# One decoder block on one core: the three late token operands of the up projection start at byte 160 of a 256-byte line, as the other four do

## The chip, the core and the metric

The kernel runs on one core of one Trainium2 chip. The metric is the device time of one execution in microseconds; the time before is the median of three runs. TensorE (PE) multiplies, and loads the stationary operand of each product with a separate weight load (PEld). VectorE (DVE), ScalarE (ACT) and GpSimd (POOL) prepare operands and take results away, and SyncE (SP) and POOL start the transfers.

## The reference, cut to what matters

One decoder block over 512 tokens of width 2048: an input projection, four heads of gated linear attention, four heads of differential attention, an output projection, and a gated MLP of width 5632 with a causal convolution of three taps.

```python
h = rmsnorm(x, attn_pre_norm);  m = token_mixer(h, w_in, ..., w_o)
x = x + rmsnorm(m, attn_post_norm)
h = rmsnorm(x, ffn_pre_norm)
up = h @ w_ffn_in                        # 2048 -> 2 * 5632
a, b = up[..., :5632], up[..., 5632:]
f = (gelu(conv3(a)) * b) @ w_ffn_out     # 5632 -> 2048
x = x + rmsnorm(f, ffn_post_norm)
```

## The kernel before, in words

Every large product is made of three: an fp32 operand is split into a rounded part (hi, written by ACT) and a rest (lo, by DVE), and hi·hi, hi·lo and lo·hi are summed in PSUM. The tokens stand as `ah` and `al` (L70, L71), 128 x (4 token tiles, 16 k tiles, 128), 32 KB in a partition each. Weights come in granules of 512 KB (`load` L96, `load_t` L817) into four buffers `raw` or four `rt`, and `granule` (L101) splits each into `whi` and `wlo` of 1024 columns, of which there are three each; in places every fourth granule goes to a spare pair, `xhi` and `xlo`. The order of the instructions on each engine is fixed when the program is built.

Which operand moves through the array and which stands in it differs by stage. In the profile's names, `bank<-A,B` has the moving operand first.

- `mm_n` (L160 to L166) in `proj_n`: the weights move, 512 columns in one piece; a slice of `ah` or `al` of 128 columns stands. It makes the value and gate parts of the input projection and the whole output projection. A granule is 24 matmuls, of which six belong to each token tile. `to_ffn` (L616) calls it in an order of its own, six matmuls for a granule and token tile.
- `mm_t` (L138 to L148) in `proj_t`: the tokens move, four blocks of 128 columns (one of each token tile, 8192 bytes apart); the weights stand. It makes queries and keys and the first of the up projection. A granule is 24 matmuls. In `to_ffn` the same function runs with two token tiles, so two blocks and 256 columns.
- `forget_gate` (L346) multiplies the moving `ah` and `al`, again four blocks, into 16 slices of `gas`, 80 columns wide and 320 bytes apart (L360, L361).
- `up_prods` (L885 to L895): the up projection, as products of 2 x 2 blocks with seven instead of eight block products (Strassen's scheme in Winograd's form). The tokens move, two blocks of 128 columns; the weights stand. Four of the seven token operands are quarters of `ah` and `al` (`a11`, `a12`, `s7`, `a22`: two blocks 8192 bytes apart). The three others, `s5`, `s2` and `s3`, are tiles of their own (L776), hi and lo each 8 KB, with the two blocks 4096 bytes apart; `up_sums` (L780) writes them. A unit (L826) has seven segments of two granules, one for each token operand, in the order y0 (`s2`), z1 (`s3`), x1 (`a12`), y1 (`s7`), the next unit's x0 (`a11`), y2 (`a22`), and the next unit's z0 (`s5`). A segment is 2 granules x 2 columns halves x 4 k tiles x 3 = 48 matmuls, and there are 20 units.
- `down_prods` (L984 to L992): the down projection, by the same scheme. The weights move, 512 columns in one piece; slices of `ah` and `al` stand. A granule is 12 matmuls; every fourth granule is `xhi`, `xlo`. `ffn_out_part` (L1091 to L1099) does the same for the last group.

All tiles are laid out by pools, one behind the other in a partition. The pool `small` (L59) stands behind `ah` and `al` and ahead of `w` (L63: `raw`, `whi`, `wlo`), `rp` (`rt`), `fa` (L727: `s5`, `s2`, `s3`, the unit's result tiles) and, in its place later, `ff`. So a byte more or less in `small` moves all that follows.

```python
ss = small.tile([P, 2], F32, name="ss2", tag="ss2")           # L216, eight buffers of 32 bytes
rp = ctx.enter_context(tc.tile_pool(name="rp", bufs=4))       # L725
fp = fa.enter_context(tc.tile_pool(name="fa", bufs=2))        # L727
for n in ("s5", "s2", "s3"):                                  # L776
    up[n] = tuple(fp.tile([P, 2, HK, P], F32R, name=f"{n}{v}", bufs=1) for v in "hl")
```

Of the kernel before, what the change touches and what calls it, by code (L numbers as in the profile page):

```python
# [9 lines left out]
F32 = mybir.dt.float32  # L10
# [7 lines left out]
P = 128  # L18
# [17 lines left out]
def hybrid_layer(ctx: ExitStack, tc: tile.TileContext, x, attn_pre_norm, w_in, w_alpha_up, b_alpha,  # L36
# [3 lines left out]
    nc = tc.nc  # L40
# [6 lines left out]
    def dma(o, i):  # L47
        return nc.sync.dma_start(out=o, in_=i)
# [10 lines left out]
    small = ctx.enter_context(tc.tile_pool(name="small", bufs=8))  # L59
# [13 lines left out]
    def bank(pool=None):  # L73
        return (pool or psa).tile([P, 512], F32, name="bank", tag="bank")
# [21 lines left out]
    def load(src, a):  # L96
        raw = wpool.tile([P, GR], F32, name="raw", tag="raw", bufs=4)
        dma(raw.rearrange("p (a b) -> p a b", a=a), src)
        return raw

    def granule(src, a, raw=None, spare=None, bufs=4):  # L101
        if raw is None:
            raw = load(src, a)
        if spare:
            hi = spare.tile([P, GR], F32R, name="xhi", tag="xhi", bufs=bufs)
            lo = spare.tile([P, GR], F32R, name="xlo", tag="xlo", bufs=bufs)
        else:
            hi = wpool.tile([P, GR], F32R, name="whi", tag="whi")
            lo = wpool.tile([P, GR], F32R, name="wlo", tag="wlo")
        act(hi, raw, AF.Copy)  # L110
        tt(lo, raw, hi.bitcast(F32), ALU.subtract)  # L111
        r = "p (a b) -> p a b"
        return hi.rearrange(r, a=a), lo.rearrange(r, a=a)

    def rsqrt_mean(ss, n, width=1):
        t = small.tile([P, width], F32, name="ms", tag="ms")
        nc.gpsimd.tensor_scalar(t, ss, 1.0 / n, EPS, ALU.mult, ALU.add)
        r = small.tile([P, width], F32, name="rs", tag="rs")
        nc.gpsimd.tensor_tensor(r, t, nhalf[:, :width], ALU.pow)
        return r  # L120
# [5 lines left out]
    def transpose_into_act(src, t, slot0, n):  # L126
        for g in range(0, n, 4):
            m = min(4, n - g)
            b = bank()
            for j in range(m):  # L130
                nc.tensor.transpose(b[:, j * P:(j + 1) * P], src[:, (g + j) * P:(g + j + 1) * P], ident)  # L131
            bv = b[:, :m * P].rearrange("p (k c) -> p k c", k=m)
            split(ah[:, t, slot0 + g:slot0 + g + m, :], al[:, t, slot0 + g:slot0 + g + m, :], bv)

    def bcast_row(tile_ap, row):
        dma(tile_ap, row.partition_broadcast(P))
# [23 lines left out]
    def mm_n(banks, t, g, w):  # L160
        for k in range(2):
            s = 2 * g + k
            st, sp = s == 0, s == KT - 1
            mm(banks[t], ah[:, t, s, :], w[0][:, k, :], start=st, stop=False)  # L164
            mm(banks[t], ah[:, t, s, :], w[1][:, k, :], start=False, stop=False)  # L165
            mm(banks[t], al[:, t, s, :], w[0][:, k, :], start=False, stop=sp)  # L166
# [17 lines left out]
    def big8(name):  # L184
        return mx.tile([P, 2048], F32, name=name, tag="big8", bufs=6)
# [8 lines left out]
    def first_half(c):  # L194
        gb = big8("gb")
        jb = mx.tile([P, 1024], F32, name="jb", tag="jb", bufs=1)
        xts = [big8("xt") for _ in range(NT)]
        H2 = [slice(1024 * i, 1024 * (i + 1)) for i in range(2)]
        H4 = [slice(512 * i, 512 * (i + 1)) for i in range(4)]
        rs, raws, w = {}, {}, {}  # L200
        banks = [bank(psm) for _ in range(NT)]
        col = C_GV + 512 * c

        def load_x(t):
            for i in range(2):
                dma(xts[t][:, H2[i]], x2[t * P:(t + 1) * P, H2[i]])

        def load_w(*gs):
            for g in gs:
                raws[g] = load(w_in3[:, 2 * g:2 * g + 2, col:col + 512], 2)  # L210

        def weights(g):
            w[g] = granule(None, 2, raws[g], spare=mx if g == 3 else None, bufs=1)

        def square(t):
            ss = small.tile([P, 2], F32, name="ss2", tag="ss2")  # L216
            for i in range(2):
                act(jb, xts[t][:, H2[i]], AF.Square, accum_out=ss[:, i:i + 1])
            sm = small.tile([P, 1], F32, name="ss", tag="ss")
            nc.gpsimd.tensor_tensor(sm, ss[:, 0:1], ss[:, 1:2], ALU.add)  # L220
            rs[t] = rsqrt_mean(sm, D)

        def scale(t, *ps):
            for i in ps:
                stt(xts[t][:, H4[i]], xts[t][:, H4[i]], rs[t], gb[:, H4[i]], ALU.mult, ALU.mult)

        def turn(t, *ps):
            for i in ps:
                transpose_into_act(xts[t][:, H4[i]], t, 4 * i, 4)

        def prods(t, *gs):
            for g in gs:
                mm_n(banks, t, g, w[g])

        load_x(0)
        bcast_row(gb[:, H2[0]], attn_pre_norm[0, H2[0]])
        load_w(0, 1, 2)
        load_x(1)
        load_w(3)
        load_x(2)  # L240
        load_x(3)
        bcast_row(gb[:, H2[1]], attn_pre_norm[0, H2[1]])
        square(0)
        scale(0, 0, 1)
        weights(0)
        turn(0, 0, 1)
        weights(1)
        weights(2)
        square(1)
        prods(0, 0, 1)  # L250
        scale(1, 0, 1)
        prods(0, 2)
        weights(3)
        turn(1, 0, 1)
        square(2)
        prods(0, 3)
        square(3)
        scale(2, 0, 1)
        prods(1, 0, 1, 2)
        turn(2, 0, 1)  # L260
        prods(1, 3)
        scale(3, 0, 1)
        prods(2, 0, 1)
        turn(3, 0, 1)
        scale(0, 2, 3)
        prods(2, 2)
        turn(0, 2, 3)
        scale(1, 2, 3)
        prods(2, 3)
        turn(1, 2, 3)  # L270
        scale(2, 2, 3)
        prods(3, 0, 1)
        turn(2, 2, 3)
        scale(3, 2, 3)
        prods(3, 2)
        turn(3, 2, 3)
        prods(3, 3)
        return banks
# [446 lines left out]
    rp = ctx.enter_context(tc.tile_pool(name="rp", bufs=4))  # L725
    fa = ExitStack()
    fp = fa.enter_context(tc.tile_pool(name="fa", bufs=2))  # L727
    ud0 = dram.tile([P, 4, S], F32, name="ud0")
    SN = ("a11", "a12", "a22", "s5", "s2", "s7", "s3")
    sd = [{n: dram.tile([P, 2, S], F32, name=f"sd{c}{n}") for n in SN} for c in range(NG // 2)]  # L730
# [460 lines left out]
```

## Time and profile before

| | us |
|---|---|
| median of 3 runs (lowest to highest) | 2177.14 (2175.53 to 2177.21) |
| the profiled execution's own time | 2177.07 |
| its span, first to last instruction | 2175.4 |
| PE busy in the span | 2140.5 (98%) |
| DVE busy | 1418.5 (65%) |
| ACT busy | 901.4 (41%) |
| POOL busy | 204.8 (9%) |

The granted clock of TensorE is 0.996 over the span. In time the stages are: the first projection up to 126 us, the mixer's projections with the attention work in their gaps up to 625, the output projection up to 845, the passage to the MLP and the first up products up to 937, the up units from 937 to 1725, the down units to 2113, and the last group to the end.

How to read it: a matmul's record in the profile is longer than the time that it keeps the array, since matmuls follow each other in a pipeline; what counts is the distance from one start to the next. In a timeline, the first column is the start in us from the span's beginning, and the second the record's length. A row of the grouped view has the line, engine, operation, tiles, shapes and count, then busy us and the mean ns of one record, then the idle time before.

### The profile page before, as it was taken

To read this page: it belongs to the slowest core of one execution; us is meant where nothing else is said; L and a number is where in the kernel's file an instruction comes from. 1 tells how busy PE (TensorE), PEld (TensorE's weight loads), DVE (VectorE), ACT (ScalarE), POOL (GpSimd) and SP (SyncE) were. 2 spreads that over 40 slices of the span, in tenths; PEclk is the share of its full clock that TensorE was granted. 3 is DMA by queue.
4 is the path that set the end of the run, shared out by engine and by line. 5 is a ranking of instruction groups with operands and counts; after the bars stand their busy time and mean duration, and the time that the engine had idled before them with its cause. 6 is when DMAs were issued, how large, how long until landed. Compare 5 with 4: busy or idle time off the path is not lost.

```text
span 2175.4 us, 31878 instructions
## 1 busy us (share of the span) xinstructions
PE 2140.5 (98%) x13009; PEld 1893.4 (87%) x13009; DVE 1418.5 (65%) x1721; ACT 901.4 (41%) x1162; POOL 204.8 (9%) x245
## 2 busy tenths in 40 slices
PE   7999999999999999999999999999999899999997
PEld 6778888787888888899999999999999788788886
DVE  5345554443444237688777786777777777888987
ACT  4233332333343224344444544444444464444433
POOL 1000000000000001011111111111011011111101
PEclk9999999999999999999999999999999999999999
DMA  6322222223224335365776757667577677576653
GB/s 212 101 71 78 78 69 78 78 78 84 77 83 167 95 126 184 126 133 129 162 169 152 163 142 181 155 144 183 140 168 181 180 212 211 167 194 174 172 157 136
DMA packets 218472, 303.83 MB, mean 140 GB/s; under 512 B 11777, under 2 KB 155573, under 8 KB 216405
## 3 DMA queue, kind: packets, MB, share of 16 engines
q1 hardware_dynamic: 165204, 238.87, 33.6%
q0 software_dynamic: 53120, 62.92, 18.6%
q8 instruction: 102, 1.67, 0.3%
q14 instruction: 46, 0.37, 0.0%
HBM read 273.97 MB, written 27.79 MB: 139 GB/s over the span
## 4 chain that ended last, share of the span: by engine, by line
PE 50%; issue 43%; POOL 3%; DVE 2%; DMA 1%; ACT 1%; POOLq 0%; SPq 0%; DVEq 0%; ACTq 0%
PE bank L164 7%; PE bank L166 7%; PE bank L165 6%; PE bank L148 5%; PE bank L146 5%; PE bank L147 5%; PE bank L991 3%; PE bank L992 3%; PE bank L990 3%; POOL rt L842 2%; POOL raw L842 2%; PE bank L413 1%; PE bank L481 1%; PE bank L512 1%; PE bank L131 1%
## 5 line engine op out<-in xcount | busy, mean ns | idle before, releaser
L111 DVE TENSOR_TENSOR wlo<-raw,whi 128x1024 fp32r<-128x1024 f32 x307 | 374.4, 1222 | 363.1 <-ACT whi L110 353.0
L110 ACT ACTIVATE whi<-raw 128x1024 fp32r<-128x1024 f32 x307 | 324.8, 1059 | 604.2 <-PE bank L166 160.3
L895 PE MATMUL bank<-ah,wlo 128*128 128x256 f32 x1280 | 353.7, 276 | 0.4 <-DVE wlo L111 0.4
L893 PE MATMUL bank<-ah,whi 128*128 128x256 f32 x1280 | 353.6, 276 | 0.0
L894 PE MATMUL bank<-al,whi 128*128 128x256 f32 x1280 | 353.4, 276 | 0.0
L111 DVE TENSOR_TENSOR wlo<-rt,whi 128x1024 fp32r<-128x1024 f32 x220 | 267.9, 1221 | 94.9 <-ACT whi L110 94.8
L110 ACT ACTIVATE whi<-rt 128x1024 fp32r<-128x1024 f32 x220 | 232.3, 1059 | 229.8 <-PE bank L894 171.5
L895 PEld LDWEIGHTS bank<-ah,wlo 128*128 128x128 f32 x1280 | 240.2, 188 | 0.8 <-DVE wlo L111 0.8
L893 PEld LDWEIGHTS bank<-ah,whi 128*128 128x128 f32 x1280 | 240.4, 188 | 0.1
L894 PEld LDWEIGHTS bank<-al,whi 128*128 128x128 f32 x1280 | 240.3, 188 | 0.1
L164 PE MATMUL bank<-whi,ah 128*128 128x512 f32 x600 | 238.4, 400 | 0.6 <-ACT ah L123 0.6
L165 PE MATMUL bank<-wlo,ah 128*128 128x512 f32 x600 | 236.5, 395 | 0.0
L166 PE MATMUL bank<-whi,al 128*128 128x512 f32 x600 | 236.3, 396 | 0.0
L146 PE MATMUL bank<-ah,whi 128*128 128x512 f32 (+1 forms) x512 | 198.0, 387 | 0.0
L147 PE MATMUL bank<-al,whi 128*128 128x512 f32 (+1 forms) x512 | 196.6, 384 | 0.0
L148 PE MATMUL bank<-ah,wlo 128*128 128x512 f32 (+1 forms) x512 | 196.6, 384 | 0.0
L991 PE MATMUL bank<-wlo,ah 128*128 128x512 f32 x420 | 164.8, 393 | 1.5 <-DVE wlo L111 1.5
L992 PE MATMUL bank<-whi,al 128*128 128x512 f32 x420 | 164.7, 393 | 0.0
L990 PE MATMUL bank<-whi,ah 128*128 128x512 f32 x420 | 156.1, 390 | 0.3 <-DVE acc L998 0.3
L166 PEld LDWEIGHTS bank<-whi,al 128*128 128x128 f32 x600 | 113.1, 189 | 25.6 <-DVE al L124 0.3
L165 PEld LDWEIGHTS bank<-wlo,ah 128*128 128x128 f32 x600 | 113.2, 189 | 24.9 <-DVE wlo L111 0.5
L164 PEld LDWEIGHTS bank<-whi,ah 128*128 128x128 f32 x600 | 113.1, 189 | 24.4 <-ACT ah L123 1.0
(250 smaller groups left out, 4103.9 us busy)
## 6 DMA issues: line engine op xcount, KB each, us to landing
raw<-in_w_in_dram SPq DMA_DIRECT2D x96, 512.0 KB, 3.8
raw<-in_w_ffn_in_dram SPq DMA_DIRECT2D x96, 512.0 KB, 4.7
raw<-in_w_ffn_out_dram SPq DMA_DIRECT2D x48, 512.0 KB, 5.8
rt<-in_w_ffn_in_dram SPq DMA_DIRECT2D x40, 512.0 KB, 6.3
rt<-in_w_ffn_in_dram POOLq DMA_DIRECT2D x40, 512.0 KB, 6.1
raw<-in_w_ffn_in_dram POOLq DMA_DIRECT2D x40, 512.0 KB, 7.0
raw<-in_w_o_dram SPq DMA_DIRECT2D x32, 512.0 KB, 3.8
rt<-in_w_ffn_out_dram SPq DMA_DIRECT2D x20, 512.0 KB, 7.2
```

Source lines behind the costliest of these rows:

```text
L110: act(hi, raw, AF.Copy)
L111: tt(lo, raw, hi.bitcast(F32), ALU.subtract)
L146: mm(o, wh, ah[:, t0:t1, kk, :], start=st, stop=False)
L147: mm(o, wh, al[:, t0:t1, kk, :], start=False, stop=False)
L148: mm(o, wl, ah[:, t0:t1, kk, :], start=False, stop=sp)
L164: mm(banks[t], ah[:, t, s, :], w[0][:, k, :], start=st, stop=False)
L165: mm(banks[t], ah[:, t, s, :], w[1][:, k, :], start=False, stop=False)
L166: mm(banks[t], al[:, t, s, :], w[0][:, k, :], start=False, stop=sp)
L893: mm(o, wh, sh[:, :, kk, :], start=start and kk == 0 and n == 0, stop=False, **NOW)
L894: mm(o, wh, sl[:, :, kk, :], start=False, stop=False, **NOW)
L895: mm(o, wl, sh[:, :, kk, :], start=False, stop=kk == HK - 1, **NOW)
L991: mm(b[j], sh[:, o:o + P], w[1][:, q, :], start=False, stop=False, **NOW)
```

## The change

`ss2` has four buffers instead of eight, which takes 4 x 32 = 128 bytes out of `small`; a tile `pad` of 80 floats, 320 bytes, which nothing reads, stands ahead of everything else in `fa` and is set to zero once by DVE. No other instruction is added, removed or moved on any engine.

```diff
@@ first_half, square
-            ss = small.tile([P, 2], F32, name="ss2", tag="ss2")
+            ss = small.tile([P, 2], F32, name="ss2", tag="ss2", bufs=4)
@@ hybrid_layer
     rp = ctx.enter_context(tc.tile_pool(name="rp", bufs=4))
     fa = ExitStack()
     fp = fa.enter_context(tc.tile_pool(name="fa", bufs=2))
+
+    pad = fp.tile([P, 80], F32, name="pad", bufs=1)
+    nc.vector.memset(pad, 0.0)
     ud0 = dram.tile([P, 4, S], F32, name="ud0")
```

On DVE, where `up_sums` begins (L791), the rows of before are these; the names in brackets are the semaphores waited for.

```order
578 L111 TENSOR_TENSOR wlo<-raw,whi 128x1024 [waits DMAHW1_49,PE_49,Activation_49]
579 L111 TENSOR_TENSOR wlo<-raw,whi 128x1024 [waits DMAHW2_49,PE_49,Activation_49]
580 L111 TENSOR_TENSOR wlo<-raw,whi 128x1024 [waits DMAHW3_49,PE_49,Activation_49]
581 L791 TENSOR_TENSOR u<-ah 128x1024 [waits DMAHW0_49,DMAHW4_49,DVE_49,PE_49]
582 L741 SCALAR_TENSOR_TENSOR u<-bank,cols,u 128x511 [waits Activation_49]
```

On DVE at the same place, the rows of the changed program (its lines are three higher from here on):

```order
579 L111 TENSOR_TENSOR wlo<-raw,whi 128x1024 [waits DMAHW2_49,PE_49,Activation_49]
580 L111 TENSOR_TENSOR wlo<-raw,whi 128x1024 [waits DMAHW3_49,PE_49,Activation_49]
581 L730 MEMSET pad 128x80 [waits DMAHW0_49,DMAHW4_49,DVE_49,PE_49]
582 L794 TENSOR_TENSOR u<-ah 128x1024
583 L744 SCALAR_TENSOR_TENSOR u<-bank,cols,u 128x511 [waits Activation_49]
```

The memset stands ahead of the first sum and has taken over its waits; the sum then waits for nothing, and what follows stands as it did.

What the two programs allot, in bytes from the start of a partition, and in brackets the remainder by 256. All further buffers of a kind follow at multiples of 4096 or 8192, and all slices that a matmul takes of one begin at multiples of 512 in it, so the remainder holds for each matmul (`gas` apart).

| tile | before | after |
|---|---|---|
| `ah`; `al` | 17056; 49824 (160) | 17056; 49824 (160) |
| `whi`; `wlo`, first buffer | 102112; 114400 (224) | 101984; 114272 (96) |
| `s5`, `s2`, `s3`, first: `s5h` | 143072 (224) | 143264 (160) |
| `xhi`, in `to_ffn` | 178016 to 190304 (96) | 177888 to 190176 (224) |
| `xhi`; `xlo`, in the down units | 192352; 196448 (96) | 192224; 196320 (224) |
| `xhi`; `xlo`, in `first_half` | 187872; 191968 (224) | 187744; 191840 (96) |
| `gas`, its slices 320 bytes apart | 167392 (224, 32, 96, 160) | 167264 (96, 160, 224, 32) |

## The prediction

> **What bounds the kernel now.** I read the page's busy times first, then the table of windows by stage, what PE waited for, the groups by line and shape, and last the timeline of PE, to take the distance from one matmul's start to the next's in each stage.
>
> ```profile
> PE 2140.5 (98%) x13009; PEld 1893.4 (87%) x13009; DVE 1418.5 (65%) x1721; ACT 901.4 (41%) x1162; POOL 204.8 (9%) x245
> 126.00:625.00 499.00, 498.54 (x2322) 406.38 (x2321) 245.59 (x471) 174.43 (x319) 29.62 (x64) 1.00 0.26 76
> 671.00:821.00 150.00, 150.00 (x658) 122.87 (x657) 49.14 (x50) 41.26 (x59) 1.49 (x4) 1.00 0.41 137
> 937.00:1713.00 776.00, 776.00 (x6676) 775.91 (x6675) 589.30 (x596) 368.12 (x401) 101.72 (x80) 1.00 0.67 158
> 1745.00:2113.00 368.00, 366.79 (x1592) 298.44 (x1591) 307.83 (x323) 177.26 (x184) 45.29 (x38) 1.00 0.69 182
> PE bank L895 <- DVE wlo L111: 0.4, 1, 0.4
> ACT whi L110 <- PE bank L894: 327.1, 226, 4.2
> ```
>
> A row of windows has the stretch, its length, then the busy time of PE, PEld, DVE, ACT and POOL, the granted clock (1.00) and the DMA share. In each stage PE is busy all the time, at the full clock; in the up units it waits once, for 0.4 us, while DVE works 589 of 776 us, and the preparation of weights waits for PE (327.1 us) and not PE for it. So the time is the number of matmuls by the distance of their starts, and whatever changes that distance goes into the time whole. The distance is not the same for equal matmuls. First rows of segments of one up unit:
>
> ```profile
> 1043.47 0.28 PE L893 MATMUL bank<-ah,whi 128*128 128x256 f32 x1
> 1048.91 0.28 PE L893 MATMUL bank<-ah,whi 128*128 128x256 f32 x1
> 1059.79 0.28 PE L893 MATMUL bank<-s5h,whi 128*128 128x256 f32 x1
> 1065.53 0.28 PE L893 MATMUL bank<-s2h,whi 128*128 128x256 f32 x1
> 1071.29 0.28 PE L893 MATMUL bank<-s3h,whi 128*128 128x256 f32 x1
> 1082.52 0.28 PE L893 MATMUL bank<-ah,whi 128*128 128x256 f32 x1
> ```
>
> The `s7` segment starts at 1043.47 and `a11` at 1048.91: 5.44 us for 48 matmuls, 113.3 ns each. From `a11` to `s5`, two segments, are 10.88 us, 5.44 each. `s5` takes 5.74, `s2` 5.76 (120.0 ns each), and `s3` with `a12` 11.23. Form, weights and stage are the same; the operands differ in their place in 256 bytes (160 against 224, the place of the weights too), in the step between their two blocks, and in their region.
>
> **Part 1: the three operands move to place 160.** If they run as the quarters of `ah` do, a unit saves 0.30 + 0.32 + 0.35 = 0.97 us, and 20 units 19.4 us. Nothing in the unit becomes late: at 38.08 instead of 39.05 us a unit, DVE's share goes from 76% to 78%. The weights that stand in the array move as well, to place 96. Matmuls in `to_ffn` show that combination, tokens at 160 and standing weights at 96 (`xlo`), beside the present one (`wlo`):
>
> ```profile
> 883.80 0.28 PE L148 MATMUL bank<-ah,xlo 128*128 128x256 f32 x1
> 886.52 0.28 PE L148 MATMUL bank<-ah,xlo 128*128 128x256 f32 x1
> 887.21 0.28 PE L148 MATMUL bank<-ah,wlo 128*128 128x256 f32 x1
> 888.57 0.28 PE L148 MATMUL bank<-ah,wlo 128*128 128x256 f32 x1
> ```
>
> Twenty-four matmuls in 2.72 us and twelve in 1.36: 113.3 ns in both. So the four quarters of `ah` lose nothing, and the three others should come to 113.3. I take 19.0 us, as the changeovers between segments may keep a little; the ends are 0 (place has nothing to do with it) and 19.4.
>
> **Part 2: the weights move from 224 to 96 where they are the moving operand.** Half of PE's time is there, and the trace has both places.
>
> ```profile
> 730.17 0.39 PE L164 MATMUL bank<-whi,ah 128*128 128x512 f32 x1
> 735.66 0.39 PE L164 MATMUL bank<-whi,ah 128*128 128x512 f32 x1
> 828.37 0.40 PE L164 MATMUL bank<-xhi,ah 128*128 128x512 f32 x1
> 829.77 0.40 PE L164 MATMUL bank<-xhi,ah 128*128 128x512 f32 x1
> 1991.69 0.39 PE L990 MATMUL bank<-whi,ah 128*128 128x512 f32 x1
> 1994.44 0.39 PE L990 MATMUL bank<-xhi,ah 128*128 128x512 f32 x1
> 1997.23 0.39 PE L990 MATMUL bank<-whi,ah 128*128 128x512 f32 x1
> ```
>
> In the output projection, `whi` at 224 takes 5.49 us for a granule of 24; six matmuls with `xhi` at 96 take 1.40, so 24 of them 5.60: 0.11 us more. In a down unit a granule of 12 takes 2.75 us from `whi` and 2.79 from `xhi`: 0.04 more. The counts are in the groups:
>
> ```profile
> L164 PE MATMUL bank<-whi,ah 128*128 128x512 f32 x600 | 238.4, 400 | 0.6 <-ACT ah L123 0.6
> L146 PE MATMUL bank<-ah,whi 128*128 128x512 f32 x448 | 180.2, 402 | 0.0
> L990 PE MATMUL bank<-whi,ah 128*128 128x512 f32 x420 | 156.1, 390 | 0.3 <-DVE acc L998 0.3
> L990 PE MATMUL bank<-xhi,ah 128*128 128x512 f32 x140 | 54.6, 402 | 7.0 <-ACT xhi L110 7.0
> L1097 PE MATMUL bank<-whi,ah 128*128 128x512 f32 x56 | 21.0, 389 | 0.0
> L164 PE MATMUL bank<-xhi,ah 128*128 128x512 f32 x40 | 16.1, 403 | 0.0
> ```
>
> Each group has two sisters of the same size. So `proj_n` has 600 x 3 / 24 = 75 granules, and loses 75 x 0.11 = 8.2 us; the down units have 420 x 3 / 12 = 105, and lose 4.2; the last group has 14, and loses 0.6. Together 13.0 us. The spare pairs go the other way, to 224: 140 x 3 / 12 = 35 granules in the down units by 0.04 are 1.4 us, and those of `to_ffn` (40 less 8 in `first_half`, by 3, in sixes: 16) by 1.40 - 1.37 are 0.5. So part 2 costs 13.0 - 1.9 = 11.1 us; its ends are 0, if `xhi` is slower for another reason than its place, and 12.5, if in the down units it is 0.05 that a granule loses.
>
> **Part 3: `mm_t`, where the tokens move and the weights stand.** The moving operand stays where it is; the weights' place goes from 224 to 96. Its pace now, and that of `gas`, whose slices stand at four places under the same moving tokens:
>
> ```profile
> 898.01 0.39 PE L146 MATMUL bank<-ah,whi 128*128 128x512 f32 x1
> 903.61 0.39 PE L146 MATMUL bank<-ah,whi 128*128 128x512 f32 x1
> 130.26 0.39 PE L360 MATMUL bank<-ah,gas 128*80 128x512 f32 x1
> 130.72 0.39 PE L360 MATMUL bank<-ah,gas 128*80 128x512 f32 x1
> 131.17 0.40 PE L360 MATMUL bank<-ah,gas 128*80 128x512 f32 x1
> 131.64 0.39 PE L360 MATMUL bank<-ah,gas 128*80 128x512 f32 x1
> ```
>
> `mm_t` takes 5.60 us for 24, as `xhi` does. In each, the moving operand lies 64 bytes below the standing one (160 to 224, 96 to 160). The faster `whi` of part 2 lies 64 above (224 to 160), and the slow `s` operands lie at the same place as the standing one. This suggests that the distance between the two operands decides, and the `gas` rows bear it out: two matmuls take 0.46 us with the slice at 32, 0.45 at 96, and 0.47 at 160, the tokens' own place. By distance, `mm_t` would go to 5.49 and its 448 x 3 / 24 = 56 granules gain 6.2 us; by the moving operand's place alone they gain 0. The `gas` rows are the nearest and lie between; I take half, 3.0 us. The two readings agree on parts 1 and 2, since there both the place and the distance come to one that the rows show.
>
> The Trainium skill (SBUF — State Buffer, section Who interferes with whom) counts two read ports for PE, one for the moving operand and one for the weight load, independent of each other. By that the standing operand's place could matter nowhere, and the sum would lack this part. The `gas` rows differ from it by 0.01 to 0.02 us in 0.46.
>
> **Part 4: the small things.** `pad` is a memset of 80 columns on DVE; the nearest is
>
> ```profile
> L298 DVE MEMSET setup<- 128x64 f32 x7 | 0.6, 112 | 0.0
> 887.18 1.23 DVE L791 TENSOR_TENSOR u<-ah 128x1024 f32<-128x1024 f32 x1 [8.62 <-PE bank L148]
> ```
>
> so about 0.1 us. It takes over the waits of the first sum of `up_sums`, before which DVE idles for 8.62 us until PE lets go, and so it delays what is queued behind it (the sums, the convolution and the next `wlo`) by 0.1 us. PE has no wait there; I count 0.1, ends 0 and 0.2. The four buffers of `ss2` serve four calls, one for each token tile, so no call waits for another: 0.
>
> **Sum.** -19.0 + 11.1 - 3.0 + 0.1 = -10.8 us. The profiled execution took 2177.07 with a span of 2175.4, 1.7 around it, and stands at the median (2177.14). 2177.1 - 10.8 = **2166.3 us**. With part 2 at 12.5 and part 3 at 0, this case ends at 2177.1 - 19.0 + 12.5 + 0.1 = 2170.7; with part 1 at 19.4 and part 3 at 6.2, at 2162.7.
>
> **The rivals.** Slower: the pace of the three operands comes from their step of 4096 bytes, or from their region, and not from their place. Then part 1 is 0 and the weights' new place costs what part 2 says: 2177.1 + 11.1 - 3.0 + 0.1 = 2185.3. It decides from the point at which a unit gains less than 8.2 / 20 = 0.41 us of the 0.97. For it speaks that no other operand of the trace has that step. Against it: `mm_t` has the step of the quarters, 8192, and is slow all the same, and within one segment of `s2` no block is faster than another.
>
> Faster still: the `xhi` granules are slow for being a pair apart from the others, and the weights stay at 5.49 and 2.75 from place 96. Then part 2 is 0: 2177.1 - 19.0 - 3.0 + 0.1 = 2155.2. For it: the trace has no `whi` at 96. Against it: the two stages that use spare pairs have them in different buffers, and both are slow.
>
> No change: neither place nor distance sets the pace, and what the rows show belongs to the tiles themselves. Then only the memset is left, 2177.2. A rule to the same end stands in the Trainium skill (TensorE: Matmul & The Clock Gate, section Wait — 56ns, not 53.3ns?): start to start is the number of columns over 2.4 GHz plus about 2.5 ns, at any address. By it 256 columns take 109 ns, and the trace has 113.3 and 120.0 for the same shape, so it doesn't hold here in this form.
>
> **Chances.** A measurement here can tell 0.2%, 4.4 us. The forecast's case has 0.58, slower 0.17, faster still 0.15, no change or gains and losses that cancel 0.10. The range takes in the forecast's case, the one faster still, a little beyond its 2155.2 as part 3 may be more than half of 6.2, and no change: 2153 to 2178, and leaves out the slower one. Faster by over 0.2% is 0.58 + 0.15 = 0.73, within 0.10, slower 0.17.
>
> **What would show it.** Right: in the changed trace, `s5`, `s2` and `s3` segments of 5.44 us; `proj_n` granules of 5.60 and down granules of 2.79 from `whi`, and of 2.75 from `xhi`; `mm_t` granules between 5.49 and 5.60, which tells distance from place. Wrong: segments of 5.76 still, or PE waiting in the up units, or `whi` granules of 5.49.

## The result, and the profile after

The changed kernel takes 2190.99 us (median of 4 runs, 2188.8 to 2191.74); the kernel before, in the same comparison, 2176.74 (median of 4, 2175.53 to 2177.21). The ratio is 1.0065, with a 95% interval of 1.0047 to 1.0082: slower, where 2166.3 was forecast. The profiled execution has a span of 2190.0 us (before 2175.4) at a granted clock of 0.995 (before 0.996). A thousandth of the span is 2 us, and in the up units both traces have 1.00, so the clock is not where the 14 us come from.

The page's first line for the changed kernel:

```profile
PE 2155.7 (98%) x13009; PEld 1904.3 (87%) x13009; DVE 1421.3 (65%) x1722; ACT 904.3 (41%) x1162; POOL 204.7 (9%) x245
```

The same number of matmuls, and PE as busy as before: they have become slower, not rarer. Where, the windows of the up units tell (the stretch, its length, busy time and count of PE, PEld, DVE, ACT and POOL, granted clock, DMA share, GB/s):

```profile
940.00:954.00 14.00, 14.00 (x125) 13.96 (x124) 13.41 (x13) 7.80 (x9) 0.00 (x0) 1.00 0.29 69
955.00:1723.00 768.00, 768.00 (x6524) 768.00 (x6523) 573.93 (x582) 359.08 (x391) 100.25 (x79) 1.00 0.67 157
```

The first 14 us hold 125 matmuls (the first and the last only in part), 113 ns each. The 768 us behind them hold 6524: 117.7 ns each, at the same clock, with PE busy throughout. The timeline of PE shows the place where it turns, and segments later on:

```profile
940.16 0.28 PE L896 MATMUL bank<-ah,whi 128*128 128x256 f32 x1
945.60 0.28 PE L896 MATMUL bank<-s5h,whi 128*128 128x256 f32 x1
954.10 0.28 PE L897 MATMUL bank<-s3l,whi 128*128 128x256 f32 x1
954.50 0.38 PE L898 MATMUL bank<-s2h,wlo 128*128 128x256 f32 x1
1064.38 0.28 PE L896 MATMUL bank<-s5h,whi 128*128 128x256 f32 x1
1070.03 0.28 PE L896 MATMUL bank<-s2h,whi 128*128 128x256 f32 x1
1103.95 0.28 PE L896 MATMUL bank<-s5h,whi 128*128 128x256 f32 x1
```

The stage opens as forecast: the `a11` segment takes 5.44 us (940.16 to 945.60), and the `s` operands behind it run at 113.3 ns as well. Between 954.10 and 954.50 lie 0.40 us in place of 0.11: a pause of 0.29. After it the `s5` segment takes 5.65 us, 117.8 ns a matmul, and so does every other: from `s5` to the next unit's `s5` are 39.57 us, seven times 5.65. Before, a unit took 39.05; forecast were 38.08. What PE waited for at 954.50 stands on DVE:

```profile
953.23 1.22 DVE L111 TENSOR_TENSOR wlo<-rt,whi 128x1024 fp32r<-128x1024 f32 x1
```

The `wlo` that the matmul reads is written from 953.23 on for 1.22 us, to 954.45.

The other stages, in the order of parts 2 and 3 of the prediction:

```profile
729.94 0.40 PE L164 MATMUL bank<-whi,ah 128*128 128x512 f32 x1
735.54 0.40 PE L164 MATMUL bank<-whi,ah 128*128 128x512 f32 x1
...
903.77 0.39 PE L146 MATMUL bank<-ah,whi 128*128 128x512 f32 x1
909.26 0.39 PE L146 MATMUL bank<-ah,whi 128*128 128x512 f32 x1
...
2004.74 0.40 PE L993 MATMUL bank<-whi,ah 128*128 128x512 f32 x1
2007.54 0.39 PE L993 MATMUL bank<-xhi,ah 128*128 128x512 f32 x1
2010.29 0.39 PE L993 MATMUL bank<-whi,ah 128*128 128x512 f32 x1
```

A granule of 24 matmuls in `proj_n` now takes 5.60 us, forecast 5.60. A granule of `mm_t` takes 5.49: the whole gain that the distance rule gave, where half was taken. A down granule takes 2.80 from `whi` (2.79) and 2.75 from `xhi` (2.75).

To split the 14.6 us, I took the time from the start of each of the 6720 matmuls of the up units to the next start, in both traces, and summed what lies above 113.3 ns: 20.3 us before, 29.7 after. So the up units lost 9.4 us where 19.0 were to be gained, and everything else lost 5.2 where 8.2 was forecast. Part 1 was off by 28 us; the 3 us elsewhere belong to part 3.

### The profile page after: what moved, and what is told of

The parts are those of the page before. It is cut to its first block, busy times and chain, and to the rows that moved or that the text cites. A ratio compares the mean times of both kernels' runs of the same rounds, so it can differ in the third digit from the quotient of the medians.

```text
span 2190.0 us, 31879 instructions
## 1 busy us (share of the span) xinstructions
PE 2155.7 (98%) x13009; PEld 1904.3 (87%) x13009; DVE 1421.3 (65%) x1722; ACT 904.3 (41%) x1162; POOL 204.7 (9%) x245
## 4 chain that ended last, share of the span: by engine, by line
PE 94%; DVE 3%; DMA 1%; ACT 1%; issue 1%; POOL 0%; SPq 0%; DVEq 0%; POOLq 0%; ACTq 0%
PE bank L897 12%; PE bank L896 12%; PE bank L898 12%; PE bank L165 6%; PE bank L164 6%; PE bank L166 6%; PE bank L994 6%; PE bank L995 6%; PE bank L993 6%; PE bank L146 5%; PE bank L148 5%; PE bank L147 5%; PE bank L413 1%; PE bank L481 1%; PE bank L512 1%
## 5 line engine op out<-in xcount | busy, mean ns | idle before, releaser
L897 PE MATMUL bank<-al,whi 128*128 128x256 f32 x1280 | 358.3, 280 | 0.0
L146 PE MATMUL bank<-ah,whi 128*128 128x512 f32 (+1 forms) x512 | 196.6, 384 | 0.0
L166 PEld LDWEIGHTS bank<-whi,al 128*128 128x128 f32 x600 | 113.1, 188 | 27.4 <-DVE al L124 0.3
```

The costliest lines, as they stand in the source:

```text
L146: mm(o, wh, ah[:, t0:t1, kk, :], start=st, stop=False)
L897: mm(o, wh, sl[:, :, kk, :], start=False, stop=False, **NOW)
```

## What the trace of before had already shown

From here on, a place is a byte address modulo 256, and the distance of a matmul's operands is the place of the moving one less that of the standing one, modulo 256: 192 for the quarters of `ah` before (tokens at 160, weights at 224, so the weights 64 above), 64 after the change (tokens at 160, weights at 96, the weights 64 below), and 0 where both lie at one place. A train is a run of matmuls one behind the other.

The same operands at the same places ran at both paces in the trace of before, in `to_ffn` (tokens at 160; `whi` at 224, `xhi` at 96; rows of every third matmul, `L146`):

```profile
844.39 0.28 PE L146 MATMUL bank<-ah,whi 128*128 128x256 f32 x1
846.43 0.28 PE L146 MATMUL bank<-ah,whi 128*128 128x256 f32 x1
...
848.88 0.28 PE L146 MATMUL bank<-ah,whi 128*128 128x256 f32 x1
853.82 0.28 PE L146 MATMUL bank<-ah,whi 128*128 128x256 f32 x1
...
859.76 0.28 PE L146 MATMUL bank<-ah,xhi 128*128 128x256 f32 x1
862.24 0.28 PE L146 MATMUL bank<-ah,xhi 128*128 128x256 f32 x1
862.84 0.28 PE L146 MATMUL bank<-ah,xhi 128*128 128x256 f32 x1
863.86 0.28 PE L146 MATMUL bank<-ah,xhi 128*128 128x256 f32 x1
```

With `whi`, 18 matmuls take 2.04 us (113.3 ns), and then 42 take 4.94 (117.6). With `xhi`, 21 take 2.48 (118.1), and right behind a gap, 9 take 1.02 (113.3). The prediction quoted rows from 883.80 to 888.57, which all lie in a fast stretch, and did not look at these, 20 to 40 us ahead of them.

Two theories came of this. **A**: at these places a train of matmuls has two paces, 113.3 and 117.8; a pause can throw it from one to the other, and it then keeps the new one. Before, the `s` operands, at the same place as the weights, ended the slow pace once in each unit; the change took them away. **B**, the rival: the weights' new place, 64 bytes below the tokens, makes 117.8 by itself, pause or not. The expectations add **C**: the `s` tiles themselves, or the step between their blocks, set their pace.

## The experiments

The edits of e1 to e4 are shown against the changed kernel, those of e5, e7 and e8 against the experiment that each names. The table counts the times from start to next start in the up units of every trace (6720 in each; those left out are pauses), and has what they sum to above 113.3 ns.

| kernel | below 116 ns | 116 to 119.5 | 119.5 to 126 | us above 113.3 |
|---|---|---|---|---|
| before | 3770 | 328 | 2618 | 20.3 |
| the changed kernel | 123 | 6593 | 1 | 29.7 |
| e1_operands_alone | 163 | 6551 | 2 | 30.0 |
| e1_again | 1652 | 5063 | 1 | 23.2 |
| e2_weights_alone | 73 | 4195 | 2447 | 36.5 |
| e3_no_pause | 267 | 6397 | 54 | 29.1 |
| e4_restart | 101 | 6533 | 82 | 30.6 |
| e5_s3_stays | 5473 | 541 | 700 | 8.4 |
| e7_spares | 5328 | 681 | 704 | 10.1 |
| e8_half_s3 | 5759 | 572 | 381 | 6.4 |

**e1_operands_alone: the three operands move, the weights stay.** 192 bytes of padding and `ss2` as before put `s5`, `s2` and `s3` at 160 and leave the weights at 224.

```diff
-            ss = small.tile([P, 2], F32, name="ss2", tag="ss2", bufs=4)
+            ss = small.tile([P, 2], F32, name="ss2", tag="ss2")
-    pad = fp.tile([P, 80], F32, name="pad", bufs=1)
+    pad = fp.tile([P, 48], F32, name="pad", bufs=1)
```

> Only the three operands move to place 160; ss2 keeps eight buffers and the weights stay at 224, 64 bytes above every token operand. Theory A (two paces at the same places: a matmul train of 256 columns runs at 113.3 ns or at 117.8 ns, a pause can throw it from one to the other, and it then stays there): the up units begin at 113.3; if the pause of 0.3 us in the first unit comes again and throws it, all segments are 5.65 us and the time is 2177 - 6 + 17 = 2188, if not 2158. Theory B (the distance alone sets the pace: 64 above gives 117.8, 64 below 113.3): 5.44 us in all segments and 2177 - 19 = 2158. Theory C (the step of 4096 bytes or the tiles themselves): s segments of 5.76 and 2177.

Measured: a median of 2176.17 over ten runs, against 2176.78 before; ratio 0.9986 (0.9957 to 1.0015). The median hides what happened: the ten lie anywhere from 2158.7 to 2186.66, spread over the whole of it (2158.7, 2159.8, 2165.6, 2173.7, 2175.4, 2177.0, 2180.9, 2181.0, 2182.5, 2186.7). The profiled one is the slowest. Its timeline at the first pause:

```profile
952.32 0.28 PE L897 MATMUL bank<-s3l,whi 128*128 128x256 f32 x1
952.71 0.38 PE L898 MATMUL bank<-s2h,wlo 128*128 128x256 f32 x1
```

From this pause on the pace is 117.8 ns (6551 of 6720, in the table), with the weights where they always were; only the last 48, behind the first 512-column matmuls of the down units, are fast again. So B alone does not hold, and neither does C: two of 6720 times are above 119.5 ns, where the `s` operands had 120.0 before. A kernel wholly in the slow pace and one wholly in the fast differ by 6720 x 4.44 ns = 29.9 us, and the ten runs fill 28.0 of it.

**e1_again: the same kernel, one execution more**, to see another of those runs.

> The kernel with the three operands alone moved, once more, for a second trace of the same program. Theory A: its time is 2158.5 plus 4.44 ns for each matmul of the up units that ran at the slow pace (up to 6720, 30 us), and the trace shows a pause of PE at each place where the pace changes to the slow one. A change of pace in a train without a pause or a change of operands would speak against it. Theory B has no reason for another time than 2158.

Measured: 2178.33, with the kernel before at 2177.72 on that chip. Its timeline of PE at two pauses, and the windows between and behind them:

```profile
952.05 0.28 PE L897 MATMUL bank<-s3l,whi 128*128 128x256 f32 x1
952.45 0.38 PE L898 MATMUL bank<-s2h,wlo 128*128 128x256 f32 x1
...
1120.86 0.28 PE L897 MATMUL bank<-al,whi 128*128 128x256 f32 x1
1121.13 0.39 PE L898 MATMUL bank<-ah,wlo 128*128 128x256 f32 x1
```

```profile
953.00:1120.00 167.00, 167.00 (x1476) 167.00 (x1475) 125.70 (x129) 77.62 (x85) 23.10 (x18) 1.00 0.71 164
1123.00:1715.00 592.00, 592.00 (x5029) 592.00 (x5028) 444.24 (x452) 278.38 (x305) 77.09 (x61) 1.00 0.67 157
```

One execution of one program: 1476 matmuls in 167 us (113.1 ns), then 5029 in 592 us (117.7), at full clock, with PE always busy and DVE and DMA no busier. The pause at 952 is as long as in the run before (0.40 against 0.39 us from start to start) and left the pace at 113; the one at 1121 is shorter and threw it. A pause can turn the pace, then, but its length to 0.01 us does not say whether it will. The expectation's sum, 2158.5 + 5063 x 4.44 ns = 2181.0, lies 2.7 us above this single time; where those are was not traced.

**e2_weights_alone: the weights move to 96, the three operands with them** (distance 0, as before).

```diff
-    pad = fp.tile([P, 80], F32, name="pad", bufs=1)
-    nc.vector.memset(pad, 0.0)
```

> Only ss2 has four buffers and there is no pad: weights and the three operands all go to place 96, so the operands again lie at the weights' own place, and the quarters of ah lie 64 above. proj_n and down granules as in the changed kernel (5.60 and 2.79), mm_t 5.50. Theory A: s segments 5.76, and after each the quarters come back to 5.44, since a change of pace resets the train: 2177 + 11 - 6 = 2182. Theory B: quarters at 5.65, 2182 + 17 = 2199. Theory C: s segments 5.76 or less, quarters open.

Measured: 2197.2 (2196.54 to 2198.76), ratio 1.0094 (1.0077 to 1.0111): B's number. Timeline of PE:

```profile
1063.06 0.28 PE L893 MATMUL bank<-s5h,whi 128*128 128x256 f32 x1
1068.80 0.28 PE L893 MATMUL bank<-s2h,whi 128*128 128x256 f32 x1
1080.68 0.28 PE L893 MATMUL bank<-ah,whi 128*128 128x256 f32 x1
1084.21 0.28 PE L893 MATMUL bank<-ah,whi 128*128 128x256 f32 x1
```

`s5` takes 5.74 us, as before, but the quarters of `ah` behind the `s` operands run at 117.7 ns (30 matmuls in 3.53 us). Theory A in its first form, which expected 2182, falls here: the operands at distance 0 end nothing by themselves. Leaving them towards weights 64 bytes above the tokens (before) leads to 113.3, and towards weights 64 below to 117.8, in every unit of both traces. Nor is it B: the first segment of the stage, ahead of any `s` operand, still takes 5.44 us (937.94 to 943.38) with the weights at 96. The run also parts the change in two: with the weights' move alone the up units sum to 36.5 us against 20.3 before, 16 us lost, of which the operands' move then takes 7 back (29.7).

**e3_no_pause: twelve extra matmuls ahead of the first up segment** give DVE the time that it lacked at 954.

```diff
+        if not lead:
+            lead.append(1)
+            for k in range(4):
+                for v in range(3):
+                    mm(b[:, 0:256].rearrange("p (t c) -> p t c", c=P), w[0][:, k, 0:P], sh[:, :, k, :],
+                       start=True, stop=True, **NOW)
...
+    lead = []
```

> The changed kernel with 12 extra matmuls of 256 columns ahead of the first segment of the up units (their sums are overwritten), 1.4 us, so that the weights of the first unit are ready before TensorE asks for them and the pause of 0.3 us at 954 us is gone. Theory A: the train stays at 113.3 through all up units, segments 5.44, 2191 - 29 + 1.4 = 2163. Theory B: segments 5.65, 2192.

Measured: 2188.85 (2184.1 to 2190.87), ratio 1.005 (1.0035 to 1.0065). By the number that speaks for B, but the timeline of PE and the windows tell another story:

```profile
969.90 0.28 PE L903 MATMUL bank<-al,whi 128*128 128x256 f32 x1
970.32 0.39 PE L904 MATMUL bank<-ah,wlo 128*128 128x256 f32 x1
```

```profile
940.00:969.00 29.00, 29.00 (x259) 29.00 (x257) 21.25 (x20) 11.53 (x13) 2.58 (x2) 1.00 0.49 114
971.00:1723.00 752.00, 752.00 (x6387) 752.00 (x6386) 563.88 (x573) 352.81 (x386) 98.61 (x77) 1.00 0.67 157
```

The pause at 954 is gone, and with it the turn there: the fast pace lasts 29 us (259 matmuls, 113 ns with the two at the edges in part) with the weights at 96. Then another granule comes late by 0.3 us (ACT had waited 5.17 us for its transfer, until 967.95), and the pace turns at that pause and stays at 117.7. Removing one pause buys the time up to the next one, and B, by which 96 is slow from the first matmul on, falls here too.

**e4_restart: one matmul of 512 columns ahead of the `s2` segment of each unit**, as a change of shape without a pause.

```diff
+        if op == "s2" and g == 0:
+            mm(b.rearrange("p (t c) -> p t c", c=P), w[0][:, 0, 0:P], ah[:, :, HK, :], start=True, stop=True, **NOW)
```

> The changed kernel with one extra matmul of 512 columns ahead of the s2 segment of each unit (its sum is overwritten), 0.23 us by 20 units. Theory A: the change of shape starts the train anew, as it did where the up units began, so that each unit runs at 113.3 from there: 2191 - 29 + 5 = 2167 if each restart ends well, more if only some do. Theory B: segments 5.65, 2196.

Measured: 2196.28 (2195.72 to 2197.37), ratio 1.0088 (1.0073 to 1.0103). Timeline of PE around the first extra matmul:

```profile
946.87 0.28 PE L898 MATMUL bank<-s5h,whi 128*128 128x256 f32 x1
947.10 0.39 PE L891 MATMUL bank<-ah,whi 128*128 128x512 f32 x1
947.67 0.28 PE L898 MATMUL bank<-s5h,whi 128*128 128x256 f32 x1
948.74 0.28 PE L898 MATMUL bank<-s5h,whi 128*128 128x256 f32 x1
```

Two matmuls ahead of it take 0.23 us, as at the fast pace, and nine behind it 1.07, 119 ns each: a change of shape turns the pace as a pause does, here to the slow side, and none of the 19 later ones turned it back (101 times below 116 ns in the whole stage, see the table). So a pause is not needed for the turn, and a restart is no cure with the weights 64 below the tokens.

**e5_s3_stays: e1 with 64 more bytes ahead of `s3`** (shown against e1), so that `s5` and `s2` move to 160 and `s3` stays at 224, the weights' own place.

```diff
+        if n == "s3":
+            fp.tile([P, 16], F32, name="pad3", bufs=1)
```

> s5 and s2 move to place 160, s3 stays at 224, the weights' own place; the weights stay at 224. Theory A (two paces, kept until a pause or a change of distance): the s3 segment of each unit runs at 120.0 and, as in the kernel before, the train comes out of it at 113.3, so that no pause can hold the slow pace for longer than a unit: s5 and s2 segments 5.44, 20 x (0.30 + 0.32) = 12 us less than before, 2164 to 2166 in every run, with little spread. Theory B (distance alone): the same mean, as 64 below gives 113.3. A kernel whose slow pace has another cause than the pause: spread as wide as where all three operands were moved alone (2159 to 2187).

Measured: 2165.54 (four runs, 2165.07 to 2166.73), ratio 0.9949 (0.9931 to 0.9967): faster than both kernels, and as steady as before. Timeline of PE:

```profile
1213.75 0.28 PE L898 MATMUL bank<-s5h,whi 128*128 128x256 f32 x1
1219.40 0.28 PE L898 MATMUL bank<-s2h,whi 128*128 128x256 f32 x1
...
1252.59 0.28 PE L898 MATMUL bank<-s5h,whi 128*128 128x256 f32 x1
1258.03 0.28 PE L898 MATMUL bank<-s2h,whi 128*128 128x256 f32 x1
1263.47 0.28 PE L898 MATMUL bank<-s3h,whi 128*128 128x256 f32 x1
1291.00 0.28 PE L898 MATMUL bank<-s5h,whi 128*128 128x256 f32 x1
```

In the unit from 1252.59 on, as in nearly all, `s5` and `s2` take 5.44 us and the unit 38.41 against 39.05: 0.64 us in 20 units are 12.8, and 11.0 were measured (2176.57 to 2165.54). In this trace a pause of 0.07 us at 1199.79 threw the pace to 117.8 as in e1, and the `s5` segment behind it takes 5.65 (1213.75 to 1219.40). It lasted to the next `s3`, at 1225, and no longer: the next `s5` is back at 5.44. So with the weights 64 above the tokens, one segment at distance 0 in a unit returns the other six to 113.3, and moving all three operands (e1) removes not only a cost of 6.7 ns a matmul but this return. In the changed kernel the weights moved too, and there distance 0 would have led to 117.7 (e2).

**e6_map: matmuls alone, at every distance.** A kernel of separate trains, each begun by a wait: moving operands at multiples of 32 bytes, standing ones at all eight distances from them, 36 matmuls of 256 columns (five trains at each of 64 pairs of places) or 24 of 512 (three at each of 24, in one piece and in four blocks).

```python
for k in range(n):
    mm(ob, st(wei[0]), mv(tok[0], k), start=k == 0, stop=False)
    mm(ob, st(wei[0]), mv(tok[1], k), start=False, stop=False)
    mm(ob, st(wei[1]), mv(tok[0], k), start=False, stop=k == n - 1)
```

> The block is left out; the output is a copy of x. Trains of 36 or 24 matmuls in the pattern hi-hi, lo-hi, hi-lo with nothing else beside them, tokens and weights at each of eight places 32 bytes apart, each train after a pause of another length: 256 columns in two blocks (all 64 pairs of places, five trains each), 512 columns in one piece and in four blocks (three places of the tokens). Theory A: at distances other than 0, trains of the same places run at 113.3 or at 117.8, by the pause before them; at 0 all run at 120. Theory B: one pace for each distance, 113.3 at 64 below, 117.8 at 64 above, 120 at 0. If the moving operand's place alone decides, rows of the map are equal whatever the weights' place.

Measured, as the mean of a train's last 24 times from start to start (18 for 512 columns), by distance:

| distance | 256 columns, ns | 512 columns, ns |
|---|---|---|
| 0 (one place) | 120.0 (the kernel's very first train aside) | 226.7 to 228.1 |
| 32 | 116.7, some 117.8 | 233.3 |
| 64 (the weights 64 below, as after the change) | 113.3 in 13 of 40 trains, 117.8 in 27 | 228.9, one of 18 at 233.3 |
| 96 | 120.0 | 233.3 |
| 128 | 118.6 to 120.0 | 231.9 to 233.3 |
| 160 | 117.2 to 120.0 | 234.1 to 234.4 |
| 192 (the weights 64 above, as before) | 113.3 in 33 of 40 trains, 117.8 in 7 | 233.3 |
| 224 | 118.3 | 233.3 |

Two trains of the same pair of places at distance 64, one behind the other (timeline of PE; in each, the fourth matmul and the thirty-fourth):

```profile
982.06 0.28 PE L74 MATMUL o<-th,wh 128*128 128x256 f32 x1
985.46 0.28 PE L74 MATMUL o<-th,wh 128*128 128x256 f32 x1
...
986.92 0.28 PE L74 MATMUL o<-th,wh 128*128 128x256 f32 x1
990.45 0.28 PE L74 MATMUL o<-th,wh 128*128 128x256 f32 x1
```

Thirty matmuls take 3.40 us in the first and 3.53 in the second. Nothing else runs on the array, no granule is late, and the two paces are there: they belong to the pair of operands. Pauses of equal length (0.76 us from start to start, for one) began trains of both kinds, so the expectation that the pause decides falls, and so does B's single pace at 64. A pace for the moving operand's place alone falls too: each place gave 113.3 at distance 192 and 120.0 at 0. The changed kernel's up units stand at 64, where the slow pace came up in 27 starts of 40; e1 stands at 192, where it came up in 7. That fits the runs, though it is not proof: the four of the changed kernel lie within 3 us, at the slow end, and those of e1 anywhere between. How often each pace comes up may also depend on the place: at the kernels' own pairs, five trains each, it was slow in all five (tokens at 160, weights at 96) and in three (weights at 224).

**e7_spares: e5, with the spare pairs at 224 too** (128 bytes of padding ahead of each; shown against e5), to take the gain that part 2 of the prediction counted for them.

```diff
+    pad5 = wp.tile([P, 32], F32, name="pad5")
+    nc.vector.memset(pad5, 0.0)
...
+    pad4 = ff.tile([P, 32], F32, name="pad4", bufs=1)
+    nc.vector.memset(pad4, 0.0)
```

> The kernel in which s5 and s2 moved and s3 stayed, and 128 bytes ahead of the spare pairs in the output projection and in the down units, so that these lie at 224 too, 64 above the standing tokens. Distance decides: xhi granules of the down units go from 2.79 to 2.75 and those of to_ffn from 1.40 to 1.37, 35 x 0.04 + 16 x 0.03 = 1.9 us, 2165.5 - 1.9 = 2163.6. If the spare pairs are slow for another reason than their place: 2165.5.

Measured: 2167.24 (2165.17 to 2168.02), ratio 0.9949 (0.9936 to 0.9962): no better than e5. The timeline of PE:

```profile
1996.74 0.39 PE L997 MATMUL bank<-xhi,ah 128*128 128x512 f32 x1
1999.48 0.39 PE L997 MATMUL bank<-whi,ah 128*128 128x512 f32 x1
```

The spare granules of the down units did reach 2.74 us, as meant. Against that stand more late granules near the end of the up units (PE waited 0.58 us for one, ahead of 1684.82) and more time in the slow pace: 10.1 us above 113.3 ns, 1.7 more than e5. Nor did the down units come out shorter: from the start of the first of their matmuls to that of the kernel's last are 449.6 us, and 448.8 in e5. The gain in the spare granules was lost elsewhere; whether the padding has to do with the late granules was not tried.

The trace has two more things to it. The first unit starts in the slow pace, and two matmuls of `s3` among those of `s2`, at 953.37 and 953.49, are enough to bring it to 113.3. And at 1123.54 two times of 119 and 128 ns in place of 113, with no wait that the profile lists, turned the pace to 117.8 for the rest of that unit.

**e8_half_s3: e7 with only the first half of `s3`, 24 matmuls a unit, at 224** (shown against e7). `s3` is split into two tiles, the second of which lies at 160, and what writes and reads it follows.

```diff
+    up3 = {1: tuple(fp.tile([P, 2, 4, P], F32R, name=f"s3b{v}", bufs=1) for v in "hl")}
+    fp.tile([P, 16], F32, name="pad3", bufs=1)
+    up3[0] = tuple(fp.tile([P, 2, 4, P], F32R, name=f"s3a{v}", bufs=1) for v in "hl")
...
```

> As the last, but of s3 only the first four k tiles (24 of the segment's 48 matmuls) lie at 224; the other four are at 160 with s5 and s2. Theory A: 24 matmuls at distance 0 are enough to bring the train back to the fast pace, the changeover to it comes inside the segment, and a unit gains another 0.16 us: 2163.6 - 3.2 = 2160.4. If the half segment doesn't bring it back: spread up to 2185.

Measured: 2164.64 (six runs, 2161.19 to 2170.95), ratio 0.9945 (0.9932 to 0.9958). Timeline of PE:

```profile
1020.96 0.28 PE L903 MATMUL bank<-s5h,whi 128*128 128x256 f32 x1
1059.20 0.28 PE L903 MATMUL bank<-s5h,whi 128*128 128x256 f32 x1
```

A unit takes 38.24 us, 0.17 less than in e5, so in this trace 24 matmuls at distance 0 return the pace as well as 48. This is the best run and it is near what was expected; the median is 4 us above, and the spread is 9.8 us against 1.7 in e5. Pauses between one return and the next could be behind that, but none of the slower runs was traced, so it is not shown. Its interval and that of e5 overlap, so the two count as equal, and e5 is the steadier.

## Why the prediction was wrong

**Part 1 (-19.0 us) failed at the step "the four quarters of `ah` lose nothing, and the three others should come to 113.3".** The size of the gain was right where it came: the first segments after the change take 5.44 us, and e5 has `s5` and `s2` at 5.44. What was wrong is that a place has one pace, and so that the weights' new place costs the quarters nothing: in e2, where only the weights' distance to the quarters is new, these run at 117.7. Once the pace had turned at 954, the 3840 matmuls of the quarters went from 113.3 to 117.8 (+17 us), and the 2880 of the three operands from 120.0 to 117.8 (-6 us); together +11 by counts and paces. The sums above 113.3 ns give 9.4, since the first 125 stayed fast, and before paid a little more at each change of operand. The term was -19.0 and came out at +9.4.

**"Nothing in the unit becomes late" failed too,** by 0.29 us. It was argued from DVE's share over a whole unit (78%), and the first unit is not like the others: its DVE is busy 13.41 of the first 14 us (window above). 0.29 us alone would be nothing; the pace that it left behind lasted for 6524 matmuls. It was the occasion and not the whole cause: without this pause (e3) the pace turned at the next one, 16 us later, and with no pause ahead of them (e2) the quarters were slow all the same from 961 us on. PE waiting in the up units was named among the signs of a wrong forecast, and it is what happened.

**The evidence was chosen from a fast stretch.** The rows of `to_ffn` for the combination of places that the change makes were the right rows to look for, but 24 matmuls in one stretch were taken for the pace of the pair. A stretch of the same pair at 118 ns stands 20 us ahead.

**Part 2 (+11.1) and part 3 (-3.0) hold in their mechanism.** Granules came out at 5.60, 2.80 and 2.75. In part 3 the distance decides and not the place: `mm_t` went to 5.49, so the term was mis-sized by half, -6.2 in place of -3.0. With that, parts 2 to 4 make 11.1 - 6.2 + 0.1 = 5.0; everything outside the up units lost 5.2. The `gas` rows, from which half was taken, misled: they change places every two matmuls and are slowest at the tokens' own place (0.47), while in the map's whole trains 512 columns are fastest at distance 0. One end of part 2 was also summed wrongly: a loss of 0.05 in place of 0.04 for 105 + 14 granules adds 1.2 to 11.1 and makes 12.3, not 12.5, so that end of the forecast lies at 2170.5. For part 3 the prediction weighed the rule of the Trainium skill (SBUF — State Buffer, section Who interferes with whom) that PE's two read ports are independent. The map differs from what was drawn from it, that the standing operand's place could matter nowhere: with all else equal, 256 columns take from 113.3 to 120.0 ns by the distance of the two operands, and the measurement decides. Whether it is the ports that make the difference is not shown.

**The rivals.** The slower one gave 2185.3, the nearest of the four, by a wrong mechanism: it had the three operands kept at 120.0 by their step of 4096 bytes, and they left 120.0. "Faster still" fell with `proj_n` at 5.60, "no change" with all of these rows. A pace that depends on what ran before was not among the cases, and a range that left out the slower one had no room for it.

**What stays open:** what in the array or the memory makes the distance matter, and what decides at a given start which of two paces a train takes. Equal pauses led to both, in e1 and in the map. For weights 64 above the tokens it is shown that the operands at distance 0 leave the train at 113.3 (before) and return it there from 117.8 (e5, e7, e8), and for weights 64 below that they do not (e2); why is not shown.

## What to carry to other kernels

Before a duration is taken from a trace as that of a place, a shape or a form, look at all its stretches: a mean over a stage, or one clean stretch, hides a pace that depends on what ran before. Where PE is the bound and always busy, divide windows by their counts at the same granted clock, since a slow pace shows in no wait and in no busy share. And a slow part may be what keeps its neighbours fast: here leaving one of the three slow operands slow (e5, 0.9949 of before, 1.7 us from lowest to highest) beat moving all three with the weights in place (e1, 0.9986, spread over 28 us).

## What the runs showed of the hardware that was not expected

- A matmul of 256 columns has two self-keeping paces, 113.3 and 117.8 ns, when its operands lie 64 bytes apart modulo 256, either way; in the changed kernel the slow one lasted over 6524 matmuls, PE never idle. At distance 0 it takes 120.0, in 39 of 40 trains. For 512 columns in one matmul, 0 is the best distance (226.7 to 228.1 ns) and 160 the worst (234.1 to 234.4). At 64 these have two paces too: 228.9, and 233.3 in one train of 18 and in e1_again, where 24 of them cut into the slow pace took 5.60 us (1717.42 to 1723.02) and in the kernel before 5.50 (1712.70 to 1718.20). So a change of shape does not always turn the pace.
- In the map it was the distance, not the place in 256 bytes, that decided which paces a pair can have: for 256 columns, the eight moving places agree within 0.2 ns at 0 (the very first train aside), 96 and 224, and at 64 and 192 no place has a pace other than 113.3 and 117.8. Which of the two comes up how often at a place is not settled by five trains each.
- A pause of 0.16 us (start to start 0.27 in place of 0.11, e1_again at 1120.86) or a single matmul of another shape (e4) was enough to turn the pace until the end of a stage or nearly so. In e7, some 20 ns over two matmuls turned it up to the next `s3`. In e5, a pause of 0.28 us at 952.43 did not turn it.
- The Trainium skill (TensorE: Matmul & The Clock Gate, section Wait — 56ns, not 53.3ns?) has start to start at the number of columns over 2.4 GHz plus about 2.5 ns. By it 512 columns would take 215.8 ns (an estimate from that page); the lowest of the map is 226.7, and it varies by distance, so the rule does not hold for these products. That it holds at any address was the prediction's own reading: the rule names no address.
